# First merge loads on staging slots, gate weights split once, gate input on SyncE, transposed probabilities on ScalarE

## The chip, the cores and the metric

One core of one Trainium2 chip runs the whole program. The metric is the device time of one execution in microseconds (us). In the profile PE is TensorE (PEld its weight loads), DVE VectorE, ACT ScalarE, POOL GpSimd and SP SyncE, whose queue carries most of the DMAs.

## The reference

One layer of a hybrid decoder over 2048 prompt tokens and 8 x 8 sample tokens, model width 1024, all in float32. Cut to what matters:

```python
z = x @ w_in                      # q, k, v, g_att | gq, gk, gv, g_gla, g_lr | r_att, r_gla
o_att = swa_prompt(q, k, v, sink, rel_table)          # window 128, 8 heads on 2 KV heads
log_a = log_sigmoid(g_lr @ w_gk_up + b_gk) / 16
o_gla, S = gla(gq * HK ** -0.5, gk, gv, log_a, s0)    # 4 heads, 128 x 256 states
o_gla = o_gla * rsqrt(mean(o_gla ** 2) + EPS) * gla_norm_w
h_att = (o_att * silu(g_att)) @ w_pa
h_gla = (o_gla * silu(g_gla)) @ w_pg
merged = sigmoid(r_att) * h_att + sigmoid(r_gla) * h_gla
x = layer_norm(ALPHA * x + merged @ w_o, ln_g, ln_b)
```

## The kernel before

Every large product is three products: each float32 operand is split in a rounded part (hi, an ACT copy) and the rest (lo, a DVE subtraction; `split`, L122, the copy at L123 and the subtraction at L124), and PE adds hi·hi, hi·lo and lo·hi in PSUM (`proj`, L202 to L213). The tokens are worked in six chunks, `CHUNKS`, of 384, 384, 384, 384, 256 and 320 columns. The order on PE is the order of the program text; on the other engines and on SP a scheduler sets it from the same program.

Phase 1 (L580 to L688) is attention, chunk by chunk. For each chunk it projects keys (`att_keys`, L363), values, four groups of queries (`att_queries`, L385), the low-rank gate input (stored to `gl_d`) and four output gates, and runs scores, softmax, transposes and the weighted sum of the blocks beside them (`att_scores`, `att_trans`, `att_out`). `att_trans` transposes the probabilities s on PE and copies the two halves from PSUM to pT: the first half by ACT (L439), the second by DVE (L437). The keys of the last chunk are also copied whole to kT (L614). PSUM slots of projections (`pd`) form a ring of three: a fourth projection waits until the first one's last reader is done.

Phase 2 (L984 to L1070) is the gated linear attention, 4 heads h, each over all chunks. A chunk starts with `gla_z` (L712): PE multiplies the gate weights wgk of the head with the gate input gin (L718), and ACT and DVE make the decay factors ga, gb, dm, em and ek from it. `gate_in` (L567) loads both: for a head's first chunk a piece of w_gk to wgk_st by SP (L572), a copy by ACT (L574) and a subtraction by DVE (L575), and for each chunk gin by the POOL queue (L577). It is called a chunk ahead, from `ahead` (L1010), behind four loads of x. For the last head the next chunk's gate product is started early (`Bn`, L1040).

Phase 3 (from L1099) is the merge: four passes (`Pass`) over the weights w_pa, w_ra, w_rg and w_pg, each with seven products i in `ORDER` on three column groups s, and four row groups p. `raw_w` loads weights to ws, `raw_x` inputs to xc or xs, `prep_w` and `prep_x` split them to wh, wl, xh and xl, and `combine` adds the PSUM results to tiles a12, a21 and fin. Phase 4 is the output product with w_o and the layer norm.

SBUF is reused between phases: the pool sb of phases 1 and 2 is closed, and the pools mb (left) and ma (right) of the merge lie on its addresses. sb has tags of fixed-size buffers: w (25 of 4 KB a partition), s, u (`unit`, NU = 24 of 1.5 KB), xst, and wst (2 of 4 KB, where weights are staged). A tile of ma or mb can be written once the last readers and writers of the sb tiles under it are done.

Of the kernel before, what the change touches and what calls it, by code (L numbers as in the profile page):

```python
# [12 lines left out]
F32 = mybir.dt.float32  # L13
# [30 lines left out]
MT = 352  # L44
MS = NT // (2 * MT)
LB = 384
NU = 24
NX = 8


# [7 lines left out]
def kernel(ctx, tc, io):  # L58
# [188 lines left out]
        nc.vector.scalar_tensor_tensor(dst[:, :T], th[:, :T], 1.0, ps, ALU.add, ALU.mult)  # L247


    stile("first")  # L250

    st, hi, lo = sb.tile([P, D], F32, tag="wst", name="wst", bufs=2), wtile(F32R, "wh"), wtile(F32R, "wl")
    wseq[0] = 1
# [34 lines left out]
        nc.gpsimd.dma_start(t, io[n])  # L288
    nc.vector.tensor_scalar(nw_h, nw_h, 0.5, None, op0=ALU.mult)
    nc.gpsimd.memset(mhalf, -0.5)  # L290
    for t in a_per + [as_per]:
        nc.gpsimd.memset(t, 0.0)

# [7 lines left out]
    def setup0():  # L301

        oneh = unit(name="oneh")
        rtab = small([33, NH], "rtab", 1)
        nc.gpsimd.memset(rtab, 1.0)
        nc.gpsimd.dma_start(oneh[:33, :LB], io["c_onehot"])
        nc.gpsimd.dma_start(rtab[:32], io["rel"])
        nc.gpsimd.dma_start(sink, io["sink"].broadcast_to([P, NH]))
        ssel = unit(name="ssel")[:NH, :2 * P].rearrange("h (a p) -> h a p", a=2)
        scol = small([NH, 1], "scol", 1)  # L310
        nc.gpsimd.dma_start(ssel, io["c_ssel"])
        nc.gpsimd.dma_start(scol, io["sink"].rearrange("a h -> h a"))
        oh = unit(F32R, "oh")[:33, :LB]
        rbh, rbl = (wtile(F32R, n).rearrange("p (h q) -> p h q", h=NH)[:33] for n in ("rbh", "rbl"))
        rt = rtab.unsqueeze(2).broadcast_to([33, NH, P])
        with tc.issue_after(pin["a"].ins), tc.issue_after(pin["d"].ins):
            nc.scalar.copy(oh, oneh[:33, :LB])
            nc.vector.tensor_copy(rbh, rt)
            nc.vector.tensor_tensor(rbl, rt, rbh.bitcast(F32), ALU.subtract)
        st1.update(oh=oh, rbh=rbh, rbl=rbl, ssel=ssel, scol=scol)  # L320
# [107 lines left out]
    def att_trans(A, bi, kv):  # L428
        first = A["kprev"] is None and bi == 0
        s = A.pop(("s", bi, kv))  # L430
        pT = wtile(name="pT").rearrange("p (a q) -> p a q", a=2)
        for hf in range(1 if first else 0, 2):
            tp = pa()
            for g in range(G):
                nc.tensor.transpose(tp[:, g * P:(g + 1) * P], s[:, g, hf * W:(hf + 1) * W], ident)  # L435
            if hf:
                nc.vector.tensor_copy(pT[:, hf], tp)  # L437
            else:
                nc.scalar.copy(pT[:, hf], tp)  # L439
        A["pT", bi, kv] = pT  # L440

    def att_out(A, bi):
# [124 lines left out]
    def gate_in(h, c):  # L567

        t0, T = CHUNKS[c]
        if c == 0:  # L570
            st = unit(name="wgk_st")[:96, :HK]
            nc.sync.dma_start(st, io["w_gk"][:, h * HK:(h + 1) * HK])  # L572
            w = R["wgk"] = unit(F32R, "wgk")[:96, :HK]
            nc.scalar.copy(w, st)  # L574
            nc.vector.tensor_tensor(w[64:], st[64:], w[64:].bitcast(F32), ALU.subtract)  # L575
        g = unit(F32R, "gin")[:96]
        nc.gpsimd.dma_start(g[:, :T], gl_d[:, t0:t0 + T])  # L577
        return g

    W1 = {}  # L580
# [380 lines left out]
        return out  # L961

    LAST = len(CHUNKS) - 1

    def chunk(h, c, gin, gv):
        t0, T = CHUNKS[c]
        last = c == LAST
        Tp = T - (NS if last else 0)
        B = dict(h=h, c=c, t0=t0, T=T, Tp=Tp, nt=Tp // P, last=last, wgk=R["wgk"], gin=gin, gv=gv, sg=[])
        gla_z(B)  # L970
        return B

# [11 lines left out]
    for h in range(GH):  # L984
        W2 = {}
        odd = h % 2

        def wt2(*key):
            if key not in W2:
                W2[key] = wget()  # L990
            return W2[key]

        for c in range(len(CHUNKS)):
            last = c == LAST
            end = h == GH - 1 and c >= LAST - 1
            if not end:
                B = chunk(h, c, gin, gvn if odd else [])
            else:
                B = Bn

            sums = [combine_load(stile)] if c else []
            if odd and c in (1, 2):
                sums.append(combine_load(lambda n: wtile(name=n)))

            def combine():
                if sums:
                    with tc.issue_after(pin["d"].ins):
                        combine_do(*sums.pop(0), nc.vector)

            def ahead():  # L1010

                nh, nx = (h, c + 1) if not last else (h + 1, 0)
                if nh == GH:
                    return None, None, None
                return tiles(load_x(nx)), gate_in(nh, nx), load_v(nh, nx) if nh % 2 else []

            if not odd:
                wv = [wt2("v", i) for i in range(4)]
                if c == 0:
                    wcap(wseq[0] + 2)  # L1020
                for i in range((B["T"] + P - 1) // P):
                    values(B, i)
                    if c == 0:
                        wload()
                    tick()
                if last:
                    wcap(wseq[0] + 4)
                    wload(2)
            xn, gin, gvn = ahead()
            if odd and not end:  # L1030
                if h < GH - 1 and c == 2:
                    wcap(wseq[0] + 6)
                for m in range(2):
                    gates(B, x, m, True)
                    if last:
                        wload()
                if 1 < c:
                    wload()
            if h == GH - 1 and LAST - 2 <= c < LAST:
                Bn = chunk(h, c + 1, gin, gvn)  # L1040
            dense(B, x, wt2("k"), gla_k, odd)
            combine()
            if not odd and last:
                wload()
            tick()
            dense(B, x, wt2("q"), gla_q, odd)
            if not odd and last:
                wload()
            tick()
            combine()  # L1050
            if end and not last:
                B["keep"] = wtile(name="keep")
                chain(B, 1, late=True)
                Bg, xg = B, x
            elif end:
                chain(B)
                for m in range(2):
                    gates(B, x, m, True)
                for m in range(2):
                    gates(Bg, xg, m, True)  # L1060
                for i in range(Bg["nt"]):
                    gla_c(Bg, i, P, i * P)
                drain()
                gla_store(Bg)
            else:
                if not odd:
                    for m in range(2):
                        gates(B, x, m, False)
                chain(B, 1 if (h if not last else h + 1) % 2 else 0)
            x = xn  # L1070
# [15 lines left out]
    ma = right.enter_context(tc.tile_pool(name="ma", bufs=1, side="right", reuse_waits="tile"))  # L1086
    T = MT
    NP4 = 4
    ORDER = (1, 2, 7, 6, 5, 3, 4)
    FINAL = {2: (0, 0), 5: (1, 1), 3: (0, 1), 4: (1, 0)}  # L1090

    def mtile(tag, n, bufs, dt=F32):
        pool = ma if tag in ("a12", "fin", "xc", "ws", "top") else mb
        return pool.tile([P, n], dt, tag=tag, name=tag, bufs=bufs)

    def toks(s, t):
# [2 lines left out]
    class Pass:  # L1099
# [7 lines left out]
        def raw_w(self, i, p):  # L1107
            out = []
            for c, k in {1: [(1, 1)], 2: [(1, 2)], 7: [(1, 1), (2, 1)], 6: [(2, 1), (2, 2), (1, 1)], 5: [],
                         3: [(1, 2)], 4: [(2, 2)]}[i]:  # L1110
                t = mtile("ws", KT // 2 * P, 11)[:, :self.kh * P]
                nc.sync.dma_start(t, self.w[c - 1, k - 1, p])
                out.append(t)
            return out
# [14 lines left out]
            return hi, lo  # L1129

        def raw_x(self, i, s):
            x = mtile("xs", 4 * T, 3) if self.kh == 4 else mtile("xc", 2 * T, 5)
            if i in (1, 2, 3):
                k, t = {1: (0, 0), 2: (1, 0), 3: (1, 1)}[i]
                if self.src is None:
# [29 lines left out]
        def combine(self, i, p, s, ps, parts):  # L1165
            acc, z = self.acc, None
            add = nc.vector.tensor_tensor
            if i == 1:
                a = acc[p, s, 12] = mtile("a12", T, 12)
                nc.scalar.copy(a, ps)  # L1170
            elif i == 2:
                z = mtile("fin", T, 6)
# [123 lines left out]

    for tag, n, bufs in (("a12", T, 12), ("fin", T, 6), ("xc", 2 * T, 5), ("ws", KT // 2 * P, 11), ("top", 640, 1),
                         ("xs", 4 * T, 3),  # L1300
                         ("a21", T, 12), ("cs", 2 * T, 4), ("xh", KT // 2 * T, 2), ("xl", KT // 2 * T, 2),
                         ("wh", KT // 2 * P, 8), ("wl", KT // 2 * P, 8)):
        mtile(tag, n, bufs, F32R if tag[1] in "hl" else F32)
# [8 lines left out]
    for n, (q, i, s) in enumerate(units):  # L1312
        if n >= 2 * len(ORDER) * MS and n % 3 == 0 and combos:
            with tc.issue_after(pin["x"].ins), tc.issue_after(pin["p"].ins):
                combine_do(*combine_load(lambda t: mtile("xc", 2 * T, 5)), nc.gpsimd)
        if n >= 3 * len(ORDER) * MS and n % 4 == 0 and len(wo) < 4:
            with tc.issue_after(pin["x"].ins), tc.issue_after(pin["a"].ins):
                wo.append(wo_load(mo, len(wo), 8))
# [226 lines left out]
```

## Time and profile before

| | |
|---|---|
| median of 3 runs | 1867.39 us (1864.09 to 1869.94) |
| the profiled execution | 1869.35 us, span 1867.6 us |
| mean granted clock of PE | 0.988 |
| busy: PE, PEld, DVE, ACT, POOL | 97%, 90%, 64%, 41%, 21% of the span |
| DMA | 386.70 MB, 207 GB/s over the span |

The span is the time from the first to the last recorded instruction. Busy shares are of the span. The chain of work that ended last consists to 85% of PE, 5% of DMA and 4% of DVE. Times in the rows below are us from the start of the span; "[5.33 <-ACT kT L614]" at a row says that the engine had been idle for 5.33 us before it, and which instruction ended that.

### The profile page before, as it was taken

The numbers are of one execution on the slowest core, as the hardware profiler recorded it, in microseconds if no ns is written. First come the engines' busy times: TensorE is split into PE (matmuls) and PEld (weight loads), VectorE is DVE, ScalarE is ACT, GpSimd is POOL, SyncE is SP. The second block draws the span as 40 slices with busy tenths as digits, with TensorE's granted clock in tenths as the row PEclk, the third lists the DMA queues.
The fourth block names the chain that finished last, engine by engine and source line by source line (L and its number), as shares of the span: only waits on it lengthen the run. The fifth ranks groups of instructions, "written<-read, shape, count | busy, mean of one in ns | idle before, by whom it ended". The sixth has DMA issues, their size and how long they took to land.

```text
span 1867.6 us, 30009 instructions
## 1 busy us (share of the span) xinstructions
PE 1810.2 (97%) x10883; PEld 1686.4 (90%) x10883; DVE 1198.0 (64%) x2468; ACT 770.2 (41%) x1733; POOL 394.4 (21%) x513
## 2 busy tenths in 40 slices
PE   8999998999999999999998989999999999999997
PEld 7998988989999998999998889999999999987886
DVE  5676776644446775444666659748656656966655
ACT  4443544533344564343545353445443543211110
POOL 2300000200011111000111223420265143631111
PEclk8999999999999999999999999999999999999998
DMA  8621223534357986444697389858887967895431
GB/s 280 215 105 39 75 106 139 176 133 144 135 196 266 337 280 228 173 153 151 235 321 241 132 265 300 285 182 282 283 313 247 308 217 245 281 317 183 157 117 40
DMA packets 194963, 386.70 MB, mean 207 GB/s; under 512 B 20653, under 2 KB 135557, under 8 KB 194800
## 3 DMA queue, kind: packets, MB, share of 16 engines
q1 hardware_dynamic: 187952, 375.39, 58.8%
q0 software_dynamic: 5712, 7.84, 1.5%
q8 instruction: 85, 1.39, 0.3%
q10 hardware_dynamic: 1152, 1.57, 0.3%
q14 instruction: 62, 0.51, 0.1%
HBM read 273.09 MB, written 112.62 MB: 207 GB/s over the span
## 4 chain that ended last, share of the span: by engine, by line
PE 85%; DMA 5%; DVE 4%; ACT 1%; issue 1%; POOL 1%; SPq 0%; DVEq 0%; POOLq 0%; ACTq 0%
PE pd L211 10%; PE pd L213 10%; PE pd L212 10%; PE pa L1339 8%; PE pa L1340 8%; PE pa L1338 8%; PE pd L226 6%; PE pd L224 6%; PE pd L225 6%; DMA cs<-tt_d 2%; PE pa L450 2%; PE pa L435 1%; PE pa L786 1%; PE pa L787 1%; PE pa L785 1%
## 5 line engine op out<-in xcount | busy, mean ns | idle before, releaser
L211 PE MATMUL pd<-x,wh 128*128 128x384 f32 (+2 forms) x1248 | 415.1, 333 | 12.7 <-ACT kT L614 5.3
L212 PE MATMUL pd<-x,wh 128*128 128x384 f32 (+2 forms) x1248 | 406.5, 326 | 0.0
L213 PE MATMUL pd<-x,wl 128*128 128x384 f32 (+2 forms) x1248 | 406.2, 325 | 0.3 <-DVE wl L124 0.3
L1338 PE MATMUL pa<-xh,wh 128*128 128x352 f32 x1176 | 381.9, 325 | 8.1 <-ACT wh L123 7.7
L1339 PE MATMUL pa<-xl,wh 128*128 128x352 f32 x1176 | 380.7, 324 | 8.9 <-DVE xl L124 8.4
L1340 PE MATMUL pa<-xh,wl 128*128 128x352 f32 x1176 | 381.4, 324 | 0.0
L211 PEld LDWEIGHTS pd<-x,wh 128*128 128x128 f32 x1248 | 239.0, 192 | 23.4 <-issue 8.9
L212 PEld LDWEIGHTS pd<-x,wh 128*128 128x128 f32 x1248 | 239.0, 192 | 1.0 <-DVE x L124 0.9
L213 PEld LDWEIGHTS pd<-x,wl 128*128 128x128 f32 x1248 | 238.4, 191 | 0.7 <-DVE wl L124 0.7
L1339 PEld LDWEIGHTS pa<-xl,wh 128*128 128x128 f32 x1176 | 223.7, 190 | 12.1 <-DVE xl L124 12.1
L1338 PEld LDWEIGHTS pa<-xh,wh 128*128 128x128 f32 x1176 | 221.7, 189 | 9.4 <-ACT wh L123 7.9
L1340 PEld LDWEIGHTS pa<-xh,wl 128*128 128x128 f32 x1176 | 221.8, 189 | 0.0
L124 DVE TENSOR_TENSOR xl<-xs,xh 128x1408 fp32r<-128x1408 f32 x63 | 110.2, 1750 | 75.0 <-ACT xh L123 44.4
L778 POOL TENSOR_SCALAR sq<-sq 128x1 f32<-128x1 f32 (+1 forms) x68 | 21.2, 312 | 549.2 <-ACT ring L777 541.2
L123 ACT CAST xh<-xs 128x1408 fp32r<-128x1408 f32 x63 | 86.5, 1373 | 104.2 <-PE pa L1340 78.3
L224 PE MATMUL pd<-woh,x 128*128 128x512 f32 x256 | 101.7, 397 | 0.7 <-ACT woh L123 0.7
L226 PE MATMUL pd<-wol,x 128*128 128x512 f32 x256 | 101.7, 397 | 0.5 <-DVE wol L124 0.5
L224 PE MATMUL pd<-wh,x 128*128 128x512 f32 x256 | 101.7, 397 | 0.0
L225 PE MATMUL pd<-woh,x 128*128 128x512 f32 x256 | 101.6, 397 | 0.0
L226 PE MATMUL pd<-wl,x 128*128 128x512 f32 x256 | 99.9, 390 | 0.0
L225 PE MATMUL pd<-wh,x 128*128 128x512 f32 x256 | 99.9, 390 | 0.0
L123 ACT CAST x<-xst 128x384 fp32r<-128x384 f32 (+5 forms) x68 | 38.2, 569 | 148.9 <-PE pd L225 117.3
(328 smaller groups left out, 3356.8 us busy)
## 6 DMA issues: line engine op xcount, KB each, us to landing
x<-xs_d SPq DMA_DIRECT2D x64, 768.0 KB, 7.1
wst<-wt SPq DMA_DIRECT2D x33, 512.0 KB, 4.2
xs<-xc_d SPq DMA_DIRECT2D x24, 704.0 KB, 5.4
cs<-tt_d SPq DMA_DIRECT2D x48, 352.0 KB, 4.9
xs<-xT SPq DMA_DIRECT2D x18, 704.0 KB, 6.4
xs_d<-x SPq DMA_DIRECT2D x16, 768.0 KB, 5.9
x<-xs_d SPq DMA_DIRECT2D x16, 704.0 KB, 6.3
ws<-w_ra SPq DMA_DIRECT2D x36, 256.0 KB, 4.4
```

Of the source, the lines that this page charges most:

```text
L123: pin["a"] = nc.scalar.copy(dst_h, src)
L124: i = eng.tensor_tensor(dst_l, src, dst_h.bitcast(F32), ALU.subtract)
L211: mm(ps, hi[:, s], xh[:, :T], start=(k == 0), stop=False)
L212: mm(ps, hi[:, s], xl[:, :T], start=False, stop=False)
L213: mm(ps, lo[:, s], xh[:, :T], start=False, stop=(k == n - 1))
L224: mm(ps, xh[:, xs], hi, start=(k == 0), stop=False)
L225: mm(ps, xl[:, xs], hi, start=False, stop=False)
L226: mm(ps, xh[:, xs], lo, start=False, stop=(k == KT - 1))
L450: mm(ot[pr, :], vb[:, pr], A["pT", bi, kv][:, hf], start=(hf == h0), stop=(hf == 1))
L1338: mm(ps, wh[:, ks], xh[:, ts], start=(k == 0), stop=False)
L1339: mm(ps, wh[:, ks], xl[:, ts], start=False, stop=False)
L1340: mm(ps, wl[:, ks], xh[:, ts], start=False, stop=(k == q.kh - 1))
```

## The change

It has five parts. (1) The sb pool's tags are reserved in another order, so that wst (and a new tile wgk) lie at its upper end, and the ma pool is laid out so that two new tiles lie there: wsp, all four weight tiles of the first merge product, loaded by one DMA of 512 KB, and xc1, the input of the first merge unit. In exchange xc has 4 buffers in place of 5, ws 10 in place of 11, and a12 is two tags of 3 and 9. (2) The gate weights of all heads are loaded once, by the POOL queue, and split once in `setup0`. (3) gin is loaded by SP, and for the last chunk of the last head one chunk earlier (gin5). (4) Both halves of pT are copied by ACT. (5) NU is 23.

```diff
-NU = 24
+NU = 23
...
-    stile("first")
+    stile("first"), wtile(), xslot(F32, "xst"), unit()
+    for n_, b_ in (("nm", G), ("sm", G), ("es", G), ("rd", G)):
+        small([P, b_], n_)
...
+    wgk = sb.tile([96, GH * HK], F32R, tag="wgk", name="wgk", bufs=1)
+    wgk_st = wtile(name="wgk_st")[:96, :GH * HK]
+    nc.gpsimd.dma_start(wgk_st, io["w_gk"])
...
         with tc.issue_after(pin["a"].ins), tc.issue_after(pin["d"].ins):
+            nc.scalar.copy(wgk, wgk_st)
+            nc.vector.tensor_tensor(wgk[64:], wgk_st[64:], wgk[64:].bitcast(F32), ALU.subtract)
             nc.scalar.copy(oh, oneh[:33, :LB])
...
-            if hf:
-                nc.vector.tensor_copy(pT[:, hf], tp)
-            else:
-                nc.scalar.copy(pT[:, hf], tp)
+            nc.scalar.copy(pT[:, hf], tp)
...
-        if c == 0:
-            st = unit(name="wgk_st")[:96, :HK]
-            nc.sync.dma_start(st, io["w_gk"][:, h * HK:(h + 1) * HK])
-            w = R["wgk"] = unit(F32R, "wgk")[:96, :HK]
-            nc.scalar.copy(w, st)
-            nc.vector.tensor_tensor(w[64:], st[64:], w[64:].bitcast(F32), ALU.subtract)
         g = unit(F32R, "gin")[:96]
-        nc.gpsimd.dma_start(g[:, :T], gl_d[:, t0:t0 + T])
+        nc.sync.dma_start(g[:, :T].bitcast(F32), gl_d[:, t0:t0 + T])
...
-                return tiles(load_x(nx)), gate_in(nh, nx), load_v(nh, nx) if nh % 2 else []
+                g = gin5.pop() if gin5 else gate_in(nh, nx)
+                return tiles(load_x(nx)), g, load_v(nh, nx) if nh % 2 else []
...
                 Bn = chunk(h, c + 1, gin, gvn)
+                if c == LAST - 2:
+                    gin5.append(gate_in(h, LAST))
...
+                if i == 1 and self.kh == 2:
+
+                    if p == 0:
+                        self.wsp = mtile("wsp", D, 1)
+                        nc.sync.dma_start(self.wsp.rearrange("q (p c) -> q p c", p=NP4), self.w[0, 0].rearrange("p q c -> q p c"))
+                    out.append(self.wsp[:, p * 2 * P:(p + 1) * 2 * P])
+                    continue
-                t = mtile("ws", KT // 2 * P, 11)[:, :self.kh * P]
+                t = mtile("ws", KT // 2 * P, WS)[:, :self.kh * P]
...
-            x = mtile("xs", 4 * T, 3) if self.kh == 4 else mtile("xc", 2 * T, 5)
+            x = mtile("xs", 4 * T, 3) if self.kh == 4 else mtile(*(("xc1", 2 * T, 1) if i == 1 and s == 0 else ("xc", 2 * T, 4)))
...
-    for tag, n, bufs in (("a12", T, 12), ("fin", T, 6), ("xc", 2 * T, 5), ("ws", KT // 2 * P, 11), ("top", 640, 1),
+    for tag, n, bufs in (("fin", T, 6), ("a12b", T, 3), ("xc", 2 * T, 4), ("ws", KT // 2 * P, WS), ("a12", T, 9),
+                         ("wsp", D, 1), ("xc1", 2 * T, 1),
```

The order on PE stays as it was. On the other engines it moves in many places; three of them follow. Line numbers of the changed kernel are its own, a few higher than before.

ACT, at the keys of the last attention chunk (kd0, kd1 and kT are read from the PSUM slot of the K projection, pT are the copies of the probabilities, s the exponentials). Before:

```order
L574 CAST wgk_3432<-wgk_st_3430 96x128 [waits DMAHW5_49,DMAHW0_49]
L439 COPY pT_3485<-pa_3486 128x512 [waits PE_49]
L419 ACTIVATE s_3498,sm_3512<-s_3498,nm_3511 128x256 [waits DVE_49,Activation_49]
L419 ACTIVATE s_3498,sm_3512<-s_3498,nm_3511 128x256 x3
L421 ACTIVATE es_3513<-es_3513 128x4 [waits DVE_49]
L439 COPY pT_3603<-pa_3604 128x512 [waits PE_49]
L123 CAST wh_3650<-wst_3648 128x1024
L369 CAST kd0_3462<-pd_3437 64x256
L370 CAST kd1_3463<-pd_3437 64x256
L374 CAST kd0_3462<-pd_3437 64x256 [waits DVE_49]
L375 CAST kd1_3463<-pd_3437 64x256
L614 COPY kT_3483<-pd_3437 128x320
```

Now:

```order
L430 ACTIVATE es_3431<-es_3431 128x4 [waits DVE_49]
L378 CAST kd0_3474<-pd_3449 64x256 [waits PE_49,Activation_49]
L379 CAST kd1_3475<-pd_3449 64x256
L445 COPY pT_3497<-pa_3498 128x512 [waits PE_49]
L445 COPY pT_3497<-pa_3504 128x512 [waits PE_49]
L383 CAST kd0_3474<-pd_3449 64x256 [waits DVE_49]
L384 CAST kd1_3475<-pd_3449 64x256
L614 COPY kT_3495<-pd_3449 128x320
L629 COPY vT_3545<-pd_3547 128x320 [waits PE_49,Pool_49]
L428 ACTIVATE s_3510,sm_3524<-s_3510,nm_3523 128x256 [waits DVE_49,Activation_49]
```

The casts of the keys and kT have moved ahead of the pT copies of their own step, and with kT ahead of the next exponentials, the pT copies after those and the weight cast wh.

ACT, in chunk 1 at the first queries (qa_906 and qb_907 before, qa_923 and qb_924 now, both read the PSUM slot of the first query projection). Before:

```order
L390 ACTIVATE qa_906<-pd_881 64x384 [waits PE_49]
L419 ACTIVATE s_919,sm_933<-s_919,nm_932 128x256 [waits DVE_49,PE_49]
L419 ACTIVATE s_919,sm_933<-s_919,nm_932 128x256 x3
L391 ACTIVATE qb_907<-pd_881 64x384 [waits PE_49,Activation_49]
L421 ACTIVATE es_934<-es_934 128x4 [waits DVE_49]
L439 COPY pT_1024<-pa_1025 128x512 [waits PE_49]
L390 ACTIVATE qa_975<-pd_950 64x384 [waits PE_49]
```

Now:

```order
L428 ACTIVATE s_936,sm_950<-s_936,nm_949 128x256 [waits DVE_49]
L428 ACTIVATE s_936,sm_950<-s_936,nm_949 128x256 x3
L430 ACTIVATE es_951<-es_951 128x4 [waits DVE_49]
L399 ACTIVATE qa_923<-pd_898 64x384 [waits PE_49,Activation_49]
L445 COPY pT_1041<-pa_1042 128x512 [waits PE_49,Activation_49]
L445 COPY pT_1041<-pa_1048 128x512 [waits PE_49]
L400 ACTIVATE qb_924<-pd_898 64x384 [waits PE_49]
L399 ACTIVATE qa_992<-pd_967 64x384 [waits PE_49]
```

qb stands behind the two copies of pT_1041 now, and it waits for PE: its buffer is one that the score matmuls of the same step read.

SP, at the first loads of the merge (S0 are loads of the GLA state, ug3_d the stores of the last head's outputs, xc, ws and the new tiles the first loads of the merge). Before:

```order
L848 DMA S0_11480<-state 128x4x256 [waits DMAHW2_49,DMAHW0_49]
L848 DMA S0_11482<-state 128x4x256 [waits DMAHW3_49,DMAHW1_49]
L820 DMA ug3_d_75<-sg_10842 128x384 [waits DVE_49]
L820 DMA ug3_d_75<-sg_10881 128x384 [waits DVE_49]
L1143 DMA xc_11705<-ua_d_71 128x2x352 [waits DMASW2_49,DVE_49,DMASW6_49,Activation_49,Pool_49]
L1112 DMA ws_11707<-w_pa 128x256 [waits DMAHW5_49,DMAHW4_49,DMASW4_49]
L1112 DMA ws_11709<-w_pa 128x256 [waits DMASW1_49,PE_49,Pool_49]
```

Now:

```order
L848 DMA S0_11477<-state 128x4x256 [waits DMAHW4_49]
L848 DMA S0_11479<-state 128x4x256 [waits DMAHW5_49]
L1155 DMA xc1_11704<-ua_d_71 128x2x352 [waits PE_49]
L1120 DMA wsp_11706<-w_pa 128x4x256
L1155 DMA xc_11708<-ua_d_71 128x2x352 [waits PE_49]
L1155 DMA xc_11710<-ua_d_71 128x2x352 [waits DMAHW6_49,DVE_49]
L1124 DMA ws_11732<-w_pa 128x256 [waits DMASW6_49,DVE_49,Pool_49]
```

The first input waited for stores of the POOL queue (DMASW) and for three engines; xc1 and wsp wait for a matmul alone. What still waits for POOL's stores is the weights of the second product.

## Rows read from the trace of the kernel before

**Rows 1.** Page, part 1: busy time of each engine.
```profile
PE 1810.2 (97%) x10883; PEld 1686.4 (90%) x10883; DVE 1198.0 (64%) x2468; ACT 770.2 (41%) x1733; POOL 394.4 (21%) x513
```
**Rows 2.** What PE waited for: us in total, times, longest.
```profile
PE pa L1338 <- ACT wh L123: 7.7, 1, 7.7
PE pd L211 <- ACT kT L614: 5.3, 1, 5.3
...
PE pd L718 <- DMA gin<-gl_d: 4.4, 1, 4.4
...
PE pd L211 <- DVE ek L751: 2.3, 1, 2.3
...
PE pa L785 <- ACT ak L123: 1.4, 1, 1.4
```
**Rows 3.** Stretches: length, engines' busy us, then PE clock, DMA share, GB/s.
```profile
323.70:328.60 4.90, 4.86 (x18) 4.86 (x19) 0.84 (x2) 1.19 (x4) 0.37 (x2) 0.50 0.00 0
700.00:712.00 12.00, 9.32 (x63) 8.61 (x62) 7.33 (x21) 4.46 (x15) 3.19 (x7) 1.00 0.87 275
1025.10:1028.30 3.20, 3.20 (x15) 3.20 (x16) 0.55 (x1) 2.48 (x4) 0.00 (x0) 0.50 1.05 395
1082.40:1086.40 4.00, 3.92 (x12) 3.54 (x13) 2.92 (x6) 2.50 (x7) 0.00 (x0) 0.51 1.04 370
100.00:320.00 220.00, 218.41 (x1434) 195.36 (x1432) 164.32 (x411) 102.01 (x318) 10.23 (x35) 1.00 0.27 96
```
**Rows 4.** Timeline of ACT, 303 to 330 us: start, duration, instruction.
```profile
308.72 0.19 ACT L421 ACTIVATE es<-es 128x4 f32<-128x4 f32 x1
...
319.44 0.36 ACT L369 CAST kd<-pd 64x256 fp32r<-64x256 f32 x1
...
323.27 0.42 ACT L614 COPY kT<-pd 128x320 f32<-128x320 f32 x1
```
**Rows 5.** Chain that ended last, 700 to 712 us: start, duration, piece.
```profile
698.31 8.29 DMA wgk_st<-w_gk
```
**Rows 6.** Timeline of POOL and PE, 1019 to 1026 us.
```profile
1019.68 0.59 POOL L577 DMA_DIRECT2D gin<-gl_d  x1
...
1025.09 0.64 PE L718 MATMUL pd<-gin,wgk 96*128 96x320 f32 x1 [4.37 <-DMA gin<-gl_d]
```
**Rows 7.** Chain that ended last, 1070 to 1086 us.
```profile
1076.10 2.02 DMA ug_d<-sg
...
1078.20 3.11 DMA xc<-ua_d
```
**Rows 8.** Timeline of ACT and DVE, 1080 to 1083 us.
```profile
1081.34 0.78 ACT L123 CAST xh<-xc 128x704 fp32r<-128x704 f32 x1 [7.00 <-DMA xc<-ua_d]
...
1082.15 0.89 DVE L124 TENSOR_TENSOR xl<-xc,xh 128x704 fp32r<-128x704 f32 x1 [6.08 <-ACT xh L123]
```
**Rows 9.** Timeline of PE and DVE, 28 to 32 us.
```profile
28.97 0.41 PE L330 MATMUL pa<-oh,rbh 33*128 33x384 f32 x1 [0.82 <-DVE rbh L318]
...
29.44 1.22 DVE L319 TENSOR_TENSOR rbl<-rtab,rbh 33x1024 fp32r<-33x1024 f32 x1
```
**Rows 10.** Timeline of ACT, DVE and PE, 88 to 100 us.
```profile
90.23 0.49 ACT L391 ACTIVATE qb<-pd 64x384 fp32r<-64x384 f32 x1
...
94.80 0.59 ACT L439 COPY pT<-pa 128x512 f32<-128x512 f32 x1 [3.85 <-PE pa L435]
...
95.84 0.68 DVE L413 TENSOR_TENSOR s<-pa,bias 128x512 f32<-128x512 f32 x1
...
95.99 0.34 PE L211 MATMUL pd<-x,wh 128*128 128x384 f32 x1
...
96.55 0.55 DVE L392 SCALAR_TENSOR_TENSOR qa<-pd,qa 64x384 fp32r<-64x384 f32 x1
```
**Rows 11.** Line L439 (ACT's copies of pT): durations min/median/max, and who waited.
```profile
L439 ACT COPY pT<-pa x30: 567/587/592, 94.8 to 388.1; 128x512 f32<-128x512 f32 x30
...
  POOL gin L577: 9.2, 1
```

More of the change, by code (lines that the diff above doesn't have):

```diff
@@ L247, in gate @@
         nc.vector.scalar_tensor_tensor(dst[:, :T], th[:, :T], 1.0, ps, ALU.add, ALU.mult)
-    stile("first")
+    stile("first"), wtile(), xslot(F32, "xst"), unit()
+    for n_, b_ in (("nm", G), ("sm", G), ("es", G), ("rd", G)):
+        small([P, b_], n_)
+    small([P, 3], "e1"), small([P, NB], "e8", 2), small([P, 1], "sq"), small([33, NH], "rtab", 1), small([NH, 1], "scol", 1)
     st, hi, lo = sb.tile([P, D], F32, tag="wst", name="wst", bufs=2), wtile(F32R, "wh"), wtile(F32R, "wl")
@@ L963 @@
     LAST = len(CHUNKS) - 1
+    gin5 = []
     def chunk(h, c, gin, gv):
@@ L968, in chunk @@
         Tp = T - (NS if last else 0)
-        B = dict(h=h, c=c, t0=t0, T=T, Tp=Tp, nt=Tp // P, last=last, wgk=R["wgk"], gin=gin, gv=gv, sg=[])
+        B = dict(h=h, c=c, t0=t0, T=T, Tp=Tp, nt=Tp // P, last=last, wgk=wgk[:, h * HK:(h + 1) * HK], gin=gin, gv=gv, sg=[])
         gla_z(B)
@@ L1088 @@
     NP4 = 4
+    WS = 10
     ORDER = (1, 2, 7, 6, 5, 3, 4)
@@ L1092, in mtile @@
     def mtile(tag, n, bufs, dt=F32):
-        pool = ma if tag in ("a12", "fin", "xc", "ws", "top") else mb
+        pool = ma if tag in ("a12", "a12b", "fin", "xc", "xc1", "ws", "wsp") else mb
         return pool.tile([P, n], dt, tag=tag, name=tag, bufs=bufs)
@@ L1168, in combine @@
             if i == 1:
-                a = acc[p, s, 12] = mtile("a12", T, 12)
+                a = acc[p, s, 12] = mtile(*(("a12b", T, 3) if s == 0 and p < 3 else ("a12", T, 9)))
                 nc.scalar.copy(a, ps)
@@ L1314 @@
             with tc.issue_after(pin["x"].ins), tc.issue_after(pin["p"].ins):
-                combine_do(*combine_load(lambda t: mtile("xc", 2 * T, 5)), nc.gpsimd)
+                combine_do(*combine_load(lambda t: mtile("xc", 2 * T, 4)), nc.gpsimd)
         if n >= 3 * len(ORDER) * MS and n % 4 == 0 and len(wo) < 4:
```

## The prediction

> **What bounds the kernel now.** The first part of the page comes first: TensorE (PE) is busy for 1810.2 us, 97% of the span [rows 1]. So only two things can be gained: its idle time, 57.4 us (1867.6 less 1810.2), and time in which it works at half clock. Work that is taken from or given to another engine counts only where PE then waits more or less. The second view is therefore PE's list of waits [rows 2]. Four single waits stand out there that this change touches: 7.7 us for the first converted weights of the merge (ACT wh), 5.3 for the copy of the keys kT in the last attention chunk, 4.4 for the load of a gate input gin, and 2.3 for ek, which is computed from a gate. Third come the stretches behind those waits [rows 3]. After the waits of 5.3, 4.4 and 7.7 us PE was granted 0.50, which is 1.2 GHz, for 4.9, 3.2 and 4.0 us; in the stretch around the wait of 2.3 us it kept 1.00, 2.4 GHz. What ran at the lower level would take half as long at the higher one, so these three stretches hold 2.4, 1.6 and 2.0 us more. The same view shows what lies over the attention phase: from 100 to 320 us PE is busy 218.41 of 220, while DVE has 164.3 and ACT 102.0.
>
> **The change, part by part.**
>
> *Keys of the last chunk (about 314 to 328 us).* ACT finished its exponentials at 308.9 us (308.72 + 0.19), but the casts of the keys began at 319.44 and kT at 323.27 [rows 4]. They stood behind two more groups, the next exponentials and a weight cast, and behind DVE's weight subtraction. The PSUM slot that kT frees is the one that PE's next projection wants at 318.42 (323.75 less 5.33). In the new order both first casts stand right behind the exponentials that end at 308.9, and the four subtractions, the other casts and kT follow, with two copies of 0.59 us between. Some eight operations of 0.36 to 0.6 us, partly on two engines, put kT at about 313, five microseconds before it is wanted. The 5.3 go, and 4.9 us at half clock shrink to 2.4: −7.7. Bounds: −5.3 if the clock falls all the same, −8.0 with all.
>
> *Gate weights, split once.* Per head the load, the cast and the subtraction go. For head 2 the load alone lay on the chain of waits for 8.29 us, because DMA was busy there [rows 5]; the wait that it caused was 2.3. All of it goes, since nothing else near there ends as late: −2.3, bounds −1.0 (x or gin next) and −2.5. The copies and subtractions of the other heads caused no wait; they cost nothing now and save nothing.
>
> *Gate input by SP, the last one a chunk earlier.* POOL issued the load that PE waited for only at 1019.68, behind the norm's power on POOL; PE began at 1025.09 after 4.37 us [rows 6]. On SP it is asked for before the chunk's K projection, some 10 us earlier, so it lands before PE asks at 1020.7: −4.4. ACT's copies of ak, which cost PE 1.4 us a little later [rows 2], hang on the gate's own chain from there; they may take back as much, so the bound above is −3.0. Below, −6.0 if the 1.6 us of clock come too. I take −4.4, since the ak wait speaks against more. The Trainium skill, page "DMA: Bandwidth & Descriptors", section "Issuing engines are not separate DMA queues", says that all issuers share the same 16 DMA engines, so that issuing elsewhere saves only the time to initiate. By that rule the move of 24 loads is worth nothing and this term is 0; it stands among the rivals. It bears on the queue, not on the earlier place in the program, which the row shows to be what was late.
>
> *First loads of the merge.* The x load was issued at 1078.20, after a store of POOL's that ran until 1078.12, and took 3.11 us [rows 7]. ACT had nothing to do from 1074.34 (1081.34 less 7.00), DVE from 1076.07 (1082.15 less 6.08) [rows 8]. In the new order that load and one load for all four weights wait for a matmul of the last gate alone and stand behind the state loads, some 25 us before they are used. Then ACT casts x from 1074.3 to 1075.1, DVE subtracts from 1076.1 to 1077.0, and PE's second matmul starts there, not at 1083.14 (0.66 after 1082.47): −6.1. PE's idle time is then near 2 us, as in the stretch that kept its clock, so 4.0 us at half shrink to 2.0: −8.0 together. Bounds: −4.2 if DVE takes the subtraction behind other work, −9.6 if no idle time is left.
>
> *Start.* PE already waits for DVE there (0.82 us for rbh) [rows 9], and the subtraction for the gate weights now stands ahead of rbh on DVE. It has 32 rows of 512; rbl, 33 rows of 1024, took 1.22, so I take 0.7 as an estimate: +0.7. Bounds 0 and +2.0: the 196 KB load runs beside the first weights.
>
> *Copies of pT on ACT.* 32 copies at 0.587 us [rows 11] make 19 us more for ACT, and DVE loses as many. ACT goes from 46% to about 51% in that phase, under PE's cover: 0, bounds −1.0 and +3.0.
>
> *One unit buffer less.* One place shows: in chunk 1 the cast qb of the first queries, at 90.23 before [rows 10], now comes behind two pT copies and waits for a score matmul, just ahead of PE's projection at 95.99, that frees its buffer. The copies hold ACT from 94.80 until about 96.0, the cast takes 0.49, and DVE, with a score addition of 0.68 and qa of 0.55 ahead of it, needs another 0.55 for qb: the PSUM slot comes free at about 97.5, and PE wants it at 95.99. +1.5, bounds 0 and +2.5. Nothing hides it; PE stands.
>
> *Tiles of the merge.* One ws and one xc buffer less let loads go later, but converted weights lie ready ahead of their use: 0, bounds 0 and +3.0 at the most.
>
> **The sum.** −7.7 −2.3 −4.4 −8.0 +0.7 +1.5 = −20.2 us, against the profiled execution's 1869.35, which is 2.0 above the median of the runs shown: from the median 1867.39 that gives **1847.2**. The bounds together reach from −27.1 to −3.0, that is from 1840.3 to 1864.4.
>
> **Rivals.**
>
> *A: the stalls come back one step later.* A chain that is freed in one place waits in the next: ACT's ak, DVE behind the last outputs, or a clock that falls although the wait is shorter. For it speaks that each stall has a second engine close behind (ak 1.4). Against it: five microseconds of slack at kT. If the three clock stretches (6.0) and half of the merge (3) and of the gin wait (2) stay: 1847.2 + 11 = 1858, or any value from 1853.
>
> *B: the merge's loads are not early after all*, because the new tiles lie on memory that some late reader still holds, so the change doesn't do what it says there: +8.0, 1855. Against it stands the order, in which they wait for one matmul of PE's.
>
> *C: the gin move is worth nothing*, as the rule above has it: +4.4, 1851.6, inside the forecast's own spread.
>
> *D: ACT becomes the bound of attention.* Each of the 32 added copies delays the transposes' use by its 0.587: +19, 1866, no change. Against it: half of ACT's time is idle there.
>
> *E: slower. SP works its list in order, and a gin that waits for a buffer holds the x loads behind it.* On POOL one gin waited 9.2 us for a pT copy [rows 11], and no one minded; on SP the x loads behind it would come that much later. One such wait costs at most 9.2; it decides from the third on, when 27.6 us outweigh the gain: with four, 1847.2 + 36.8 = 1884. Against it: in the new order a gin stands mostly behind x loads which themselves wait for PE's reading of the last chunk, later than the buffers come free.
>
> **How the numbers follow.** About 0.3%, 5.6 us, is what a measurement of this kernel can tell from no change. Forecast with C: 0.52, with 1842 to 1853 as its own range. A: 0.24. B: 0.08. Better than the forecast's range, down to 1840 and a little below: 0.06. D: 0.05. E: 0.05. Faster by over 0.3% means below 1861.8: all of the forecast, B and the better case, and A but for an eighth, 0.87. The same: D and that eighth, 0.08. Slower: E, 0.05. The range takes A and B in and leaves out D, E and the ends: 1839 to 1860.
>
> **What would show it.** In the profile of the changed kernel PE's waits should no longer name kT, gin or ek, and the wait for wh should be near 2 us and name DVE's xl. The granted clock should be 1.00 around 320 us and in the first merge units. New should be a wait of 1 to 2 us at about 96 us for DVE's qb, and a start that is 0.7 us later. The forecast is wrong if a wait of over 3 us stands at any of the four places, or if x loads on SP show waits behind gin.

## The result, and the profile after

The changed kernel takes 1852.89 us (median of 4 runs, 1848.82 to 1855.22), the kernel before beside it 1868.66 us (4 runs, 1864.09 to 1870.97). The ratio is 0.9916, with a 95% interval of 0.9890 to 0.9943. It is faster by 15.8 us; 20.2 were forecast, and 1847.2 as the time. The time lies within the range, at the border between the forecast's own range (up to 1853) and rival A's (from 1853). The profiled execution took 1853.14 us, its span 1851.4, its mean granted clock 0.991.

Page of the changed kernel, part 1 [rows 1]:

```profile
PE 1806.5 (98%) x10883; PEld 1684.5 (91%) x10883; DVE 1177.9 (64%) x2433; ACT 784.3 (42%) x1762; POOL 381.6 (21%) x490
```

PE's idle time fell from 57.4 to 44.9 us (1851.4 less 1806.5), and 3.7 us of its busy time went as well. What PE waited for, changed kernel (us in total, times, longest) [rows 2]:

```profile
PE pa L1352 <- DVE xl L124: 9.3, 8, 2.2
...
PE pa L785 <- ACT ak L123: 3.1, 1, 3.1
...
PE pd L211 <- DVE qb L402: 1.5, 1, 1.5
...
PE pa L1351 <- DVE fin L1185: 0.8, 1, 0.8
...
PE pa L1351 <- ACT wh L123: 0.6, 1, 0.6
```

kT, gin and ek are gone from the list, and wh is 0.6. New at the places of the change are qb, which the prediction names, a longer ak, which it allows for, and fin, which it doesn't name. PE's order is the same in both kernels, 10883 instructions, so the start of each can be set against the start of the same one before. The difference of the two starts is called the distance here. How it grew, stretch by stretch (times of the run before; a minus is a gain):

| stretch | expected us | measured us |
|---|---|---|
| start, to 60 us | +0.7 | +1.9 |
| chunk 1, qb, 94 to 105 | +1.5 | +1.8 |
| last chunk, kT, 312 to 330 | −7.7 | −7.8 |
| head 2, ek, 698 to 706 | −2.3 | −2.6 |
| gin and ak, 1010 to 1045 | −4.4 | −3.8 |
| merge start, 1070 to 1090 | −8.0 | −6.0 |
| merge, 1090 to 1376 | 0 | −2.6 |
| merge, second pass, 1376 to 1400 | 0 | +3.2 |
| behind PE's last matmul | 0 | −1.9 |
| all other stretches | 0 | +1.6 |
| sum, of the span | −20.2 | −16.2 |

PE at the places in question, timeline of the changed kernel (start, duration, instruction, the idle time before it):

```profile
99.51 0.44 PE L211 MATMUL pd<-x,wh 128*128 128x384 f32 x1 [1.50 <-DVE qb L402]
...
1014.22 0.39 PE L718 MATMUL pd<-gin,wgk 96*128 96x320 f32 x1
...
1024.44 0.58 PE L785 MATMUL pa<-gv,ak 128*128 128x256 f32 x1 [3.08 <-ACT ak L123]
...
1066.06 0.43 PE L1351 MATMUL pa<-xh,wh 128*128 128x352 f32 x1 [0.59 <-ACT wh L123]
1067.61 0.42 PE L1352 MATMUL pa<-xl,wh 128*128 128x352 f32 x1 [1.12 <-DVE xl L124]
...
1361.33 0.40 PE L1351 MATMUL pa<-xh,wh 128*128 128x352 f32 x1 [0.81 <-DVE fin L1185]
1362.77 0.43 PE L1352 MATMUL pa<-xl,wh 128*128 128x352 f32 x1 [1.04 <-DVE xl L124]
```

Stretches of the changed kernel (length, busy time of PE, PEld, DVE, ACT, POOL, then PE's clock, DMA share, GB/s) [rows 3]:

```profile
316.00:330.00 14.00, 14.00 (x96) 12.60 (x96) 8.94 (x22) 9.56 (x25) 2.10 (x6) 1.00 0.22 75
1019.00:1024.00 5.00, 2.36 (x21) 2.16 (x19) 3.17 (x10) 2.97 (x7) 0.35 (x1) 0.99 1.00 349
1023.90:1027.30 3.40, 2.86 (x12) 2.86 (x13) 3.23 (x12) 1.32 (x7) 0.61 (x1) 0.50 0.47 179
...
1068.20:1071.60 3.40, 3.40 (x13) 3.40 (x13) 1.96 (x6) 1.33 (x4) 0.00 (x0) 0.51 0.69 207
```

The last attention chunk is clean: PE is busy without a gap, at 2.4 GHz. The first gate product of the last chunk (L718) comes at 1014.22 and waits for nothing. But PE waits 3.08 us for ak instead, and runs at 1.2 GHz for 3.4 us behind that. At the merge the wait shrank to 0.59 and 1.12 us, as forecast, and still the clock fell for 3.4 us.

### The profile page after: what moved, and what is told of

It reads as the page before. It is cut to its first block, busy times and chain, and to the rows that moved or that the text cites. A ratio compares the mean times of both kernels' runs of the same rounds, so it can differ in the third digit from the quotient of the medians.

```text
span 1851.4 us, 29966 instructions
## 1 busy us (share of the span) xinstructions
PE 1806.5 (98%) x10883; PEld 1684.5 (91%) x10883; DVE 1177.9 (64%) x2433; ACT 784.3 (42%) x1762; POOL 381.6 (21%) x490
## 3 DMA queue, kind: packets, MB, share of 16 engines
q10 hardware_dynamic: 1152, 1.57, 0.3%
```

## The experiments

Each kernel was one execution, beside one of the kernel before, unless rounds are named. One execution doesn't decide about 4 us (the last section says why), so the experiments are read stretch by stretch, with the distance used above.

**1. pT's second half on DVE again.**

```diff
-            nc.scalar.copy(pT[:, hf], tp)
+            if hf:
+                nc.vector.tensor_copy(pT[:, hf], tp)
+            else:
+                nc.scalar.copy(pT[:, hf], tp)
```

> The changed kernel with the second half of pT copied by DVE again. My theory: that part is worth nothing by itself, and the wait of 1.5 us in chunk 1 comes from the unit buffer that is missing, so it stays: time as the changed kernel, 1853 within 2. Rival: the pT copies that stand ahead of qb on ACT make that wait; then it is gone and 1.5 to 2 us are gained (1851). Second rival: the copies on ACT are what freed the keys of the last chunk; then PE waits some 5 us for kT again near 320 us and the time is 1860.

Measured: 1847.29 us (before 1865.09). The distance is +4.0 at 105 us and +4.0 at 300, against +3.6 and +4.1 in the changed kernel. kT goes all the same, and the wait for qb is 1.6. So the copies of pT neither make nor remove the stalls, and rival D is refuted. They aren't free, though: between 105 and 300 us the distance grows by 0.5 in the changed kernel and in experiments 2 to 11, which all have both copies on ACT, and by 0.0 in this one and in experiment 12. All of it arises at one place, at eight transposes of PE. Changed kernel, then this one:

```profile
288.41 1.50 PE L444 MATMUL pa<-ident,s 128*128 128x128 f32 x8
```

```profile
288.79 1.04 PE L444 MATMUL pa<-ident,s 128*128 128x128 f32 x8
```

**2. gin on the POOL queue again**, its early place kept.

```diff
-        nc.sync.dma_start(g[:, :T].bitcast(F32), gl_d[:, t0:t0 + T])
+        nc.gpsimd.dma_start(g[:, :T], gl_d[:, t0:t0 + T])
```

> The changed kernel with all gin loads on the POOL queue again, the last one still a chunk earlier. Theory: a gin load that waits for its buffer holds the POOL queue, and the keys of the last attention chunk come late for that reason; the order on ACT then has kd0 and kT behind two groups of copies and a weight cast again, PE waits 5 us for kT near 320 us and loses another 2.4 to the clock: 1853 + 7.5 = 1860. Rival, as in the prediction: the queue move is worth nothing, 1853 within 2, no wait for kT.

Measured: 1857.01 us. The wait for kT is back. Timeline of ACT in this kernel:

```profile
324.03 1.07 ACT L445 COPY pT<-pa 128x512 f32<-128x512 f32 x2 [4.02 <-PE pa L444]
324.99 1.06 ACT L123 CAST wh<-wst 128x1024 fp32r<-128x1024 f32 x1
325.93 0.37 ACT L378 CAST kd<-pd 64x256 fp32r<-64x256 f32 x1
...
329.77 0.42 ACT L614 COPY kT<-pd 128x320 f32<-128x320 f32 x1
```

and of PE:

```profile
330.25 0.64 PE L211 MATMUL pd<-x,wh 128*128 128x320 f32 x1 [5.82 <-ACT kT L614]
```

The casts of the keys stand behind the next copies and the weight cast, as before the change [rows 4]. In the changed kernel ACT's timeline reads:

```profile
312.16 0.35 ACT L378 CAST kd<-pd 64x256 fp32r<-64x256 f32 x1
...
312.91 1.07 ACT L445 COPY pT<-pa 128x512 f32<-128x512 f32 x2
...
316.31 0.42 ACT L614 COPY kT<-pd 128x320 f32<-128x320 f32 x1
```

Between 312 and 330 us the distance changes by −0.4 here, by −7.8 in the changed kernel. So without the gin line the kT term is gone: it comes through the order that the scheduler gives ACT once 24 loads leave POOL's queue. (No kernel made this move alone.) At gin's own place, 1010 to 1045 us, both gain 3.8: there the queue is worth nothing, as rival C had it. The Trainium skill, page "DMA: Bandwidth & Descriptors", section "Issuing engines are not separate DMA queues", says that the choice of the issuing engine saves only the time to initiate. The 3.8 us with either queue agree with it; of the order on other engines it doesn't speak. At the end of the kernel the queue is worth another 1.9 us (see "Not in the sum" below).

**3. gin of the last chunk in its late place**, on SP.

```diff
-                if c == LAST - 2:
-                    gin5.append(gate_in(h, LAST))
```

> The changed kernel with gin on SP but the last chunk's load in its old place in the program. Theory: the early place is what removed the wait near 1014 us; PE waits some 4 us for gin there again, and the wait for ak of 3.1 us goes back to 1.4: net +3 (1856). Rival: SP alone suffices, since POOL was late only through its norm work; then no wait for gin and 1853.

Measured: 1854.09 us. PE waits for gin, and half clock follows; PE's timeline and a stretch of this kernel:

```profile
1019.33 0.64 PE L718 MATMUL pd<-gin,wgk 96*128 96x320 f32 x1 [6.76 <-DMA gin<-gl_d]
```

```profile
1015.70:1022.50 6.80, 3.17 (x14) 3.17 (x15) 2.56 (x5) 2.43 (x4) 0.00 (x0) 0.50 1.01 369
```

From 1010 to 1045 us the distance grows by 0.7 instead of shrinking by 3.8. The early place is worth 4.5 us, and it is what removes the wait.

**4. Gate weights per head again.**

```diff
-            nc.scalar.copy(wgk, wgk_st)
-            nc.vector.tensor_tensor(wgk[64:], wgk_st[64:], wgk[64:].bitcast(F32), ALU.subtract)
...
+        if c == 0:
+            st = unit(name="wgk_st")[:96, :HK]
+            nc.sync.dma_start(st, io["w_gk"][:, h * HK:(h + 1) * HK])
+            w = R["wgk"] = unit(F32R, "wgk")[:96, :HK]
+            nc.scalar.copy(w, st)
+            nc.vector.tensor_tensor(w[64:], st[64:], w[64:].bitcast(F32), ALU.subtract)
```

> The changed kernel with the gate weights loaded and split per head again. Theory: PE waits some 2.3 us for ek near 703 us again, and the start is 1 us shorter, since DVE has no subtraction ahead of rbh: net +1.4 (1854). Rival: the two more unit buffers in use at the last attention chunk bring back a wait for kT of several us (1858 or more).

Measured: 1846.91 us. Between 698 and 706 us only 0.4 is gained instead of 2.6, as expected. But the start costs nothing: the distance at 60 us is −0.1, where the changed kernel has +1.9. The split "once" gives 2.2 at head 2 and takes 2.0 at the start: in sum, nothing. (The start differs from execution to execution, see experiment 8.)

**5. The merge's memory and loads as before**: one `a12`, 11 ws, 5 xc, no wsp and no xc1, the rest changed.

```diff
-                if i == 1 and self.kh == 2:
...
-                t = mtile("ws", KT // 2 * P, WS)[:, :self.kh * P]
+                t = mtile("ws", KT // 2 * P, 11)[:, :self.kh * P]
...
+    for tag, n, bufs in (("a12", T, 12), ("fin", T, 6), ("xc", 2 * T, 5), ("ws", KT // 2 * P, 11), ("top", 640, 1),
```

> The changed kernel with the first merge loads and the merge's tiles as before (no xc1, no wsp, 5 xc, 11 ws, one a12 tag); the sb pool keeps its new order. Theory: PE waits some 7 us again at the start of the merge, so it is 6 us behind the changed kernel from there; near 1361 us, where the changed kernel waits 2.6 us in three pieces for stores of fin, it waits less, since one more ws buffer lets SP go on to the stores: about 1853 + 6 - 2.5 = 1856 to 1857. Rival: the new order of the sb pool alone lets the old tiles load early; then no wait of 7 us and 1851. Second rival: the wait near 1361 is the way these DMAs fall, not the buffers; then it stays and the time is 1859.

Measured: 1861.23 us (before 1871.33). The wait for wh is back with 7.5 us, and from 1070 to 1090 us the distance changes by −0.1 instead of −6.0. From 1376 to 1400 it doesn't change, where the changed kernel loses 3.2. So part (1) of the change gives 6 us at the merge's start and takes 3 of them in its second pass; how far the second number holds is seen in experiment 6.

**6. A ring of buffers for the merge**: after its first use wsp serves as an eleventh ws, and xc1 as a fifth xc.

```diff
+    def xcnew():
+        ring[0] += 1
+        return mtile("xc1", 2 * T, 1) if ring[0] % 5 == 1 else mtile("xc", 2 * T, 4)
...
-                t = mtile("ws", KT // 2 * P, WS)[:, :self.kh * P]
+                t = (mtile("wsp", D, 1) if len(out) == 1 and p % 2 == 0 else mtile("ws", KT // 2 * P, WS))[:, :self.kh * P]
```

> The changed kernel in which the tile of the first weights is used again as an eleventh buffer (for the short-lived second operand of a weight sum, every other row group) and xc1 as the fifth xc buffer. Theory: the waits near 1361 us (0.8 + 1.0 + 0.7) come from the buffers that are missing and go: 2 us gained from there on (1851). Rival: they come from the load on the DMA queues; no change.

Measured: 1849.35 us. The waits in the second pass are gone (−0.2 from 1376 to 1400 us). SP's queue shows why. Changed kernel (start, duration, DMA issues):

```profile
1342.85 9.22 SPq L1124 DMA_DIRECT2D ws<-w_rg  x6
1352.12 0.42 SPq L1217 DMA_DIRECT2D tt_d<-fin  x1
```

With the ring:

```profile
1343.95 4.74 SPq L1130 DMA_DIRECT2D ws<-w_rg  x4
1348.78 0.38 SPq L1223 DMA_DIRECT2D tt_d<-fin  x1
```

The chain of waits of the changed kernel names what released one of these loads (start, duration, piece):

```profile
1349.95 1.29 POOL ws L1133
1351.24 0.02 issue
1351.26 0.33 SPq L1124
```

L1133 is POOL's addition of two weight tiles, the last reader of a ws buffer. So the weight loads, which wait for ws buffers, hold the queue; the stores of fin stand behind them, and DVE can't write the next fin until they have landed. DVE in the changed kernel:

```profile
1355.41 0.52 DVE L1185 TENSOR_TENSOR fin<-a,pa 128x352 f32<-128x352 f32 x1 [5.72 <-DMA tt_d<-fin]
1360.66 0.52 DVE L1185 TENSOR_TENSOR fin<-a,pa 128x352 f32<-128x352 f32 x1 [4.73 <-DMA tt_d<-fin]
```

PE follows at 1361.33. In this stretch the distance grows by 1.5 to 3.6 us in seven executions with 10 ws (the changed kernel twice, experiments 1 to 4 and 8), and by −0.2 to 0 in the four with eleven (5, 6, 9 and 10). Experiment 7 has 10 ws too and loses nothing (−0.2): there the six loads hold SP for 6.95 us, DVE waits 2.9 and 3.2 us for the stores, and PE not at all. So one buffer less makes the loss likely, not certain. From 1110 to 1120 us the ring loses 1.5 (1.1 in experiment 9, 1.7 in 10), which none of those seven loses; but experiment 12, without a ring, loses 1.5 there too, so whether the ring is the cause isn't shown.

**7. PE kept busy across two waits** by transposes that nobody reads, ahead of ak and of the merge.

```diff
+    def busy(n):
+        d = pa()
+        for _ in range(n):
+            nc.tensor.transpose(d[:, :P], ident, ident)
...
+        if B["h"] == GH - 1 and B["c"] == LAST - 1 and i == 0:
+            busy(26)
...
+        if n == 0:
+            busy(14)
```

> The changed kernel with 26 transposes of the identity on PE in the wait for ak near 1021 us and 14 ahead of the first merge product, written to a spare PSUM tile that nobody reads. Theory: the two half-clock stretches of 3.4 us behind these waits (1024.4 to 1027.4 and 1068.3 to 1071.7 us) come from the idle time before them; with PE busy there the clock stays at 1.00 and 1.5 + 1.7 us are gained (1850). Rival: the clock falls for another reason, or transposes of this size do not hold it; then the time is the same or up to 1 us longer.

Measured: 1853.59 us, and it tells little. The 26 transposes stood in the wrong chunk, so the wait for ak and its half clock stayed. At the merge the clock held, but it also held in experiments 4, 6, 8 and 9 without any transpose. A stretch of experiment 4:

```profile
1068.00:1070.00 2.00, 2.00 (x14) 2.00 (x13) 0.79 (x3) 0.90 (x3) 0.00 (x0) 1.00 0.86 241
```

and of the changed kernel, behind the same waits:

```profile
1068.00:1070.00 2.00, 2.00 (x9) 2.00 (x9) 1.70 (x4) 0.45 (x1) 0.00 (x0) 0.56 0.62 195
```

Yet the held clock isn't worth its 2 us. From 1070 to 1120 us the distance shrinks by 5.7 in experiment 4 and by 6.2 in the changed kernel. PE, there earlier, waits for the next operands instead. PE's timeline in experiment 4:

```profile
1082.52 0.43 PE L1353 MATMUL pa<-xh,wh 128*128 128x352 f32 x1 [0.16 <-ACT xh L123]
1083.56 0.43 PE L1354 MATMUL pa<-xl,wh 128*128 128x352 f32 x1 [0.61 <-DVE xl L124]
```

The changed kernel has no wait between 1068 and 1110 us.

**8. The split of the gate weights behind rbl**, so that neither ACT nor DVE does it ahead of rbh.

```diff
-            nc.scalar.copy(wgk, wgk_st)
-            nc.vector.tensor_tensor(wgk[64:], wgk_st[64:], wgk[64:].bitcast(F32), ALU.subtract)
...
+        with tc.issue_after(rb.ins):
+            nc.scalar.copy(wgk, wgk_st)
+            nc.vector.tensor_tensor(wgk[64:], wgk_st[64:], wgk[64:].bitcast(F32), ALU.subtract)
```

> The changed kernel with the copy and subtraction of the gate weights behind the split of the bias table in the setup. Theory: DVE's 0.68 us ahead of rbh is what the start costs; PE's wait before L339 goes from 1.5 back to 0.8 and the start is 0.7 us shorter (1852). Rival: the start is longer because the 196 KB load runs beside the first weights; then no gain.

Measured: 1850.32 us. The distance at 60 us is +2.0, no better than the changed kernel's +1.9, though DVE no longer has the 0.68 us in front of rbh that it has in the changed kernel:

```profile
28.93 0.68 DVE L325 TENSOR_TENSOR wgk<-wgk_st,wgk 32x512 fp32r<-32x512 f32 x1
29.64 0.69 DVE L327 CAST rbh<-rtab 33x1024 fp32r<-33x1024 f32 x1
```

So the order of these operations isn't what the start costs. With the one load of all gate weights the distance at 60 us was +1.2 to +3.9 in eleven executions; without it −0.1 (experiment 4) and −0.9 (experiment 12). And it arises early: at 20 us, when neither ACT (27.55) nor DVE (28.93) has touched the gate weights, it is already +0.8 to +3.6 in those eleven, and −0.1 to 0 in the two. So the start is paid for the load or for the buffer that it fills, beside the first weights and inputs, and not for the split. No kernel moved the load alone, so which of these it is stays open.

**9. Ring and late split together**, 5 rounds. The edits are those of 6 and 8.

> The changed kernel with both of the two small edits: wsp and xc1 used again as buffers in the merge, and the gate weights split behind the bias table. Theory: some 2 us near 1361 us and 0.5 at the start less than the changed kernel on the same chip: ratio between them 0.998 to 0.999, 2.5 us. Rival: both are within what two executions of one kernel differ by, since the pace of the merge's matmuls differs from run to run; no difference that shows in five rounds.

Measured: 1851.0 us (6 runs, 1845.52 to 1855.12), ratio 0.9914 (0.9896 to 0.9932). The waits in the second pass are gone, but it isn't faster than the changed kernel (experiment 11).

**10. The transposes in the right chunk**, added to 9, with the 14 ahead of the merge; 5 rounds.

```diff
+        if B["h"] == GH - 1 and B["c"] == LAST - 2 and i == 0:
+            busy(26)
```

> As e9_both, with 26 transposes on PE in the wait for ak (now in the chunk in which the wait lies) and 14 ahead of the merge. Theory: the clock stays at 1.00 behind both waits, 1.5 us less each time for ak and some of the 1.7 us for the merge, so about 2 us less than e9_both. Rival: PE's granted clock falls there all the same, or the transposes run over the end of the wait; then 0 to 1 us more.

Measured: 1853.01 us (1851.98 to 1857.58), ratio 0.9931 (0.9915 to 0.9946). Two stretches of it:

```profile
1023.90:1027.30 3.40, 3.16 (x28) 2.85 (x26) 1.71 (x9) 3.23 (x9) 0.00 (x0) 1.00 0.98 351
1032.10:1035.50 3.40, 3.33 (x15) 3.31 (x15) 1.40 (x5) 1.27 (x6) 0.55 (x2) 0.51 0.73 216
```

The clock holds where it fell in the changed kernel, and falls 8 us later, behind PE's next wait:

```profile
1031.73 0.38 PE L786 MATMUL pa<-st,qih 128*128 128x256 f32 x1 [1.70 <-ACT st L123]
```

That wait took 0.30 us in the changed kernel. By this row ACT's st, and not PE, sets the pace there, and a PE that comes earlier waits longer. From 1010 to 1045 us the distance shrinks by 2.1 here and by 4.1 in experiment 9: transposes and held clock together cost 2.0 us at this place, where a gain of 1.5 was expected.

**11. The changed kernel once more**, beside 9 and 10, 5 rounds.

> The changed kernel unaltered, beside the others on one chip. Theory: 0.9916 of the kernel before, within 0.003, and single executions spread over 5 us or so, as the pace of the merge's matmuls falls. Rival: the gain of the first measurement was in part chance; then above 0.995.

Measured: 1850.13 us (6 runs, 1846.02 to 1854.58), before 1865.67 (11 runs), ratio 0.9913 (0.9895 to 0.9930). It confirms the first result; 9 and 10 don't beat it.

**12. The kernel before with NU = 23**, nothing else.

> The kernel before with NU = 23 and nothing else. Theory: the missing unit buffer makes the wait of 1.5 us for qb in chunk 1, so it appears here near 97 us, and the waits for kT (5.3), ek (2.3), gin (4.4) and wh (7.7) stay as they were: 1870. Rival: the wait in chunk 1 comes from the other parts; then there is none here.

Measured: 1868.98 us. The wait for qb appears, 1.57 us, and from 94 to 105 us the distance grows by 1.8, as in the changed kernel: the unit buffer is its cause. kT, gin and ek stay. What nobody expected is the merge, in PE's list of waits [rows 2]:

```profile
PE pa L1338 <- ACT wh L123: 1.6, 2, 1.0
```

and in SP's timeline [rows 7]:

```profile
1059.71 0.37 SPq L1143 DMA_DIRECT2D xc<-ua_d  x1
...
1065.40 15.52 SPq L1112 DMA_DIRECT2D ws<-w_pa  x4
```

With one sb buffer fewer the merge's tiles lie elsewhere, and the first input and the first two weights are free of POOL's last stores without any new tile. The third and fourth weights are not, they hold SP until 1081 us, and 3.9 of the 7.1 us gained at the first matmul are given back by 1120 us. That speaks for addresses as what decides at this place; then part (5) of the change moves addresses as part (1) does. The addresses themselves stand in no trace.

## Why the prediction was right, and where it was off

- **Keys of the last chunk, −7.7:** −7.8, the 5.3 and the 2.4 of half clock both. The prediction read it from ACT's new order and was right about that order; it didn't say which edit makes it. It hangs on the gin line (experiment 2).
- **Gate weights, −2.3:** −2.6 at the place. **Start, +0.7:** mis-sized, +1.9, near its upper bound of 2.0. The step that failed took DVE's subtraction as the price; that is 0.68 us as estimated, but experiment 8 takes it from its place ahead of rbh and gains nothing, and the loss is there before it runs. In sum the two terms are worth 0 (experiment 4), not −1.6.
- **Gate input, −4.4:** −3.8. The wait is gone, but ak took back more than the value allowed for: 3.08 us against 1.4 [rows 2], and half clock behind it. ACT stands in its own chain there, not behind the load:

```profile
1021.20 1.28 ACT L737 ACT_TABLE_LOAD   x1 [2.02 <-issue]
...
1023.94 0.28 ACT L123 CAST ak<-aper 128x128 fp32r<-128x128 f32 x1
```

  The value lies within the term's bounds of −3.0 to −6.0, and rival A's mechanism is what took the difference. One of the prediction's own signs against itself, a wait of over 3 us at one of the four places, is just met if ak's 3.08 us, ten microseconds behind gin's product, is counted as that place.
- **First loads of the merge, −8.0:** −6.0. The 6.1 us of idle time went as worked out, with PE's second matmul behind DVE's xl. The 2.0 us of clock did not: "PE's idle time is then near 2 us, as in the stretch that kept its clock" is the sentence that failed. Behind 1.7 us of idle time the clock fell in the changed kernel (both profiled executions) and in experiments 1, 2 and 3, and held in 4, 6, 8 and 9, behind the same two waits; what decides it isn't shown. Where it held, later waits took it back. Rival B is refuted: the two loads are issued 22 us ahead of their use. SP's timeline:

```profile
1043.11 0.51 SPq L1155 DMA_DIRECT2D xc<-ua_d  x1
1043.65 0.47 SPq L1120 DMA_DIRECT2D wsp<-w_pa  x1
```

- **One unit buffer less, +1.5:** 1.50 us of wait, +1.8 in the distance; experiment 12 shows the cause.
- **Copies of pT, 0:** +0.5, within the bounds (experiment 1). Rival D, with 19 us, is refuted.
- **Tiles of the merge, 0:** mis-sized, +3.2, just beyond its bound of +3.0. That converted weights lie ahead of their use isn't what failed; the price arose on SP's queue, where stores of fin stand behind loads that wait for ws. That is rival E's mechanism in another place and with another tensor; rival E itself didn't occur, no wait names x loads behind gin.
- **Not in the sum:** −2.6 in the merge, from the pace of PE's matmuls (last section), and −1.9 behind PE's last matmul. The second is the gin line again. The last long piece of the kernel is a DRAIN of POOL, an instruction behind the last operations of the program; it starts 2.4 us after PE's end in every run. Its length is the longest of the three drains in these rows (count, then ns: shortest, median, longest); kernel before, changed kernel, and experiment 2, with gin on POOL:

```profile
L1531 POOLq DRAIN  x3: 46/102/9534, 1857.2 to 1867.3; - x3
```

```profile
L1544 POOLq DRAIN  x3: 55/102/7652, 1842.9 to 1851.1; - x3
```

```profile
L1544 POOLq DRAIN  x3: 46/106/9620, 1844.8 to 1855.0; - x3
```

  With gin on SP the time behind PE's last matmul is 10.8 to 10.9 us in all eleven executions, with gin on POOL 12.7 to 12.8 in all three (before, experiments 2 and 12).

The two biggest errors, 2.0 for the merge's clock and 3.2 at its tiles, were partly offset by these two gains. That is luck: neither was foreseen, and the 2.6 differ from execution to execution. Rival C is settled from two sides: for gin's own place it is right, for the line as a whole it is wrong by 9 us, 7.4 at kT and 1.9 at the end.

## What to carry to other kernels

When an edit moves DMAs from one engine's queue to another, read the new order of every engine: here 24 loads moved off POOL gave 7.4 us through ACT's order, 1.9 through POOL's drain at the end, and nothing at the loads' own place. A buffer taken from a ring that an in-order queue waits for can delay whatever stands behind on that queue, stores too. And don't price half clock separately where another chain stands close behind: what the clock gives, the next wait may take, as at the merge and at ak here; at kT it was paid in full.

## What was not expected of the hardware

POOL's drain at the end of the kernel grows with the DMAs that POOL issued, though the last of the 24 gin loads was issued by 1020 us: 7.58 us after 80 of them (experiment 4), 7.65 after 81 (the changed kernel), 9.53 after 104 (the kernel before), 9.62 after 105 (experiment 2). That is about 0.08 us for each, an estimate from these four. What the drain does in that time isn't shown.

PE's merge matmuls of 352 columns run at one of three paces, at a granted clock of 1.00 and without idle time: 72 of them take 11.44, 11.52 or 11.60 us, by the starts of the first in each 72. The pace stays for many groups, and in these traces it changed only where PE had waited. Stretches of the same time without a wait show it by PE's count. The kernel before:

```profile
1220.00:1270.00 50.00, 50.00 (x313) 50.00 (x312) 25.64 (x36) 18.75 (x28) 14.98 (x13) 1.00 0.55 175
```

the changed kernel:

```profile
1220.00:1270.00 50.00, 50.00 (x315) 50.00 (x314) 36.60 (x61) 21.23 (x30) 14.15 (x12) 1.00 0.66 209
```

experiment 3:

```profile
1220.00:1270.00 50.00, 50.00 (x317) 50.00 (x316) 36.24 (x59) 20.30 (x31) 14.17 (x12) 1.00 0.62 196
```

Over the merge's 49 groups the slowest and the quickest pace lie 7.8 us apart (49 times 0.16). The profiled kernel before ran mostly at 11.60, the changed one at 11.52 and then 11.60, its second profiled execution mostly at 11.44. That fits the spread of 6 to 10 us among runs of one kernel, so a single execution can't tell 4 us. Only profiled executions show the pace, so that it makes this spread is likely and not shown. What sets the pace wasn't found.
